# Turning input rows by DMA in two planes of 16-bit halves, in a hybrid attention and convolution layer

## The chip, the core and the metric

The kernel runs on one core of a Trainium2 chip, as one launch. The core has TensorE (matmuls, here also transposes), VectorE and ScalarE (element-wise work), GpSimd, and SyncE, which only issues DMAs. Each engine works through its own instruction list in order and waits at semaphores for the others. The metric is the device time of one execution in microseconds (us); lower is better.

## The reference

One layer on x of shape (1, 2048, 1024), all in float32:

```
h  = rms_norm(x, attn_norm_g)
z  = h @ w_in                     # q (512) k (128) v (128) gate_b gate_c xc (512 each)
q, k = rms_norm(q), rms_norm(k)   # per head of 64
A  = swa_sink_attention(q, k, v, sinks)      # window 128, 8 heads, 2 kv heads
Cv = gate_b * short_conv(gate_c * xc, conv_w)  # causal, 3 taps
x  = x + concat(rms_norm(A), rms_norm(Cv)) @ w_out
hm = rms_norm(x, mlp_norm_g)
x  = x + square(relu(hm @ w_up)) @ w_down      # 1024 -> 4096 -> 1024
```

## The kernel before

All products keep float32 accuracy by splitting each operand into a high part that TensorE takes at full rate and a low part (the remainder): three matmuls per product, high by high, high by low, low by high. ScalarE makes the high part (a copy with rounding), VectorE the low part (a subtraction).

The work comes in three stages. In the **mixers** (up to about 690 us) the 2048 positions are taken in four chunks of 512 rows, a chunk in four tiles of 128. For a chunk: projection to q, k, v; attention for the four tiles; the convolution branch in two halves (`conv_pair`, j = 0 and 1, each with products for gate_c, xc and gate_b); output projection in two halves (first the convolution's columns, then the attention's). Then come the **up projection** and the **down projection** over all rows, with a seven-product scheme for 2x2 blocks.

The order of the mixers is made by hand. `besides` is a generator: each `yield` ends one small piece of a chunk's convolution, output projection and preparation of the next chunk. The attention code calls `fill(n)`, which runs n such pieces; the table `FILL` holds the counts for each chunk, `PRIO` holds offsets to the priorities with which a scheduler then orders instructions on each engine. So attention's steps on ScalarE and VectorE are covered by filler matmuls on TensorE.

`prepare` makes the next chunk's operand h, which must have the model dimension on partitions. It loads a tile of 128 rows (`xt`, buffers for two), takes the sum of squares on ScalarE (`norm_stats`), the reciprocal root on GpSimd, scales on VectorE (`scaled`); then `transposed` turns it on TensorE, four 128x128 blocks into one PSUM bank (tag "tr", one buffer), and splits the bank into the high part (L310, ScalarE) and the low part (L311, VectorE) of h. It runs beside the first half of the output projection: after each piece of `prepare` come three pieces of the output projection (`STEPS`). The last chunk has no next one, so there are three such preparations, in chunks 0, 1 and 2, of 4 tiles each.

Of the kernel before, what the change touches and what calls it, by code (L numbers as in the profile page):

```python
# [10 lines left out]
I32 = mybir.dt.int32  # L11
AF = mybir.ActivationFunctionType
# [55 lines left out]
PC = (2, 1)  # L68

# [8 lines left out]
LATE_RSTD = (  # L78
    (3, 3),
    (2, 2),  # L80
)
# [5 lines left out]
PRIO = (  # L87
# [5 lines left out]
)  # L93

FILL = (
# [4 lines left out]
)  # L100
# [4 lines left out]
def hymba_layer(  # L105
# [168 lines left out]
    last_sum = [None]  # L274

# [23 lines left out]

    def transposed(xt, dst, t, name, tag="tr"):  # L300

        for kk in range(0, KD, 4):
            with ahead(9):
                pt = bank(tag, f"pt_{name}_{kk}")
                for j in range(4):
                    nc.tensor.transpose(pt[:, j * P : (j + 1) * P], xt[:, (kk + j) * P : (kk + j + 1) * P], ident)
                p3 = pt.rearrange("p (k t) -> p k t", k=4)
                dh = dst[0][:, kk : kk + 4, t * P : (t + 1) * P]
                dl = dst[1][:, kk : kk + 4, t * P : (t + 1) * P]
                nc.scalar.copy(dh, p3)  # L310
                nc.vector.tensor_tensor(dl, p3, dh.bitcast(F32), op=ALU.subtract)  # L311
            yield
# [87 lines left out]
    def prepare(src, r0, gb, dst, name):  # L400

        xs = []

        def fetch(t):
            xt = row("xt", f"xt_{name}_{t}", 2)
            nc.sync.dma_start(xt, src[r0 + t * P : r0 + (t + 1) * P, :])
            with ahead(8):
                norm(xt, gb, f"{name}_{t}")
                xs.append(xt)
# [227 lines left out]
    with tc.tile_pool(name="mix_small", bufs=1) as mix_small, tc.tile_pool(name="mix", bufs=1) as mix:  # L637
# [193 lines left out]
        def attn_rstd(b, sqa, dst):  # L831
            pa = bank("tr", f"pa_b{b}")
            nc.tensor.matmul(pa[:, :1], sqa[:, :P], mean, start=True, stop=True)
            ms = small.tile([P, 1], F32, tag="ms", name=f"ms_b{b}", bufs=2)
            nc.vector.tensor_copy(ms, pa[:, :1])
            rsqrt(dst, ms)

        def conv_pair(c, h, j, yt, ssc):
# [30 lines left out]
            for i in range(2):  # L869
                ct = 2 * j + i  # L870
                ps = bank("mm", f"px_{nm}_{i}")
                yield from group(hl, ps, i)
                u = gc[i]
                with ahead(10):
                    nc.gpsimd.tensor_copy(u[:, :2], halo[:, ct, :])
                    nc.vector.tensor_tensor(u[:, 2 : CH + 2], ps, u[:, 2 : CH + 2], op=ALU.mult)
                    nc.gpsimd.tensor_copy(halo[:, ct, :], u[:, CH : CH + 2])
                    y = pool.tile([P, CHP], F32, tag="s2", name=f"y_{nm}_{i}", bufs=4)[:, :CH]
                    nc.vector.tensor_scalar(y, u[:, :CH], cw[:, ct, 0:1], None, op0=ALU.mult)
# [9 lines left out]
            for i in range(2):  # L889
# [4 lines left out]
                with ahead(10):  # L894
# [3 lines left out]
                    nc.scalar.copy(yh[:, 0], y)  # L898
# [28 lines left out]
        def out_projection(c, half, ys, rs, x1):  # L927

            for dh in range(2):
# [11 lines left out]
                for t, i in order:  # L941
# [17 lines left out]
                    if i < NCT - 1:  # L959
                        yield  # L960
                        continue
                    with ahead(11):
# [15 lines left out]
        def besides(c, before, h, yt, rc, x1, h_next, z_next):  # L978
# [3 lines left out]
            blocks = x_blocks() if c + 1 == NCHUNK else None  # L982
            for j in range(2):
# [12 lines left out]
            if c + 1 < NCHUNK:  # L996
                h_next += parts(pool, "h", f"h{c + 1}")
                steps = prepare(xf, (c + 1) * CH, g_row[0], h_next, f"a{c + 1}")
            else:
                steps = range(PC[0] + 1)  # L1000
            for i, _ in enumerate(steps):
                yield
                for j in range(STEPS):
                    next(out, None)
                    yield
                    if (i, j) == PC:
                        pc = bank("tr", f"pc{c}")
# [603 lines left out]
```

## Time and profile before

| | |
|---|---|
| runs | 1914.98, 1916.66, 1916.91 us; median 1916.66 |
| profiled execution | span 1913.4 us from the first to the last instruction; the page gives no other time of its own |
| TensorE matmuls | 8930, busy 1907.7 us |
| VectorE, ScalarE, GpSimd busy | 1202.7, 829.4, 274.4 us |
| granted TensorE clock | 1.000 over the core's span |
| DMA | 413.80 MB, mean 216 GB/s |

The profile is that of one execution. A line like `L310 ACT CAST h_h<-pt_a` names the code line, the engine (PE is TensorE, PEld its weight loads, DVE VectorE, ACT ScalarE, POOL GpSimd, SP SyncE), the operation, and what it writes and reads. Groups give total busy time and the mean length of one in ns. Busy shares average over stages with different limits, so the stage is looked at by itself.

### The profile page before, as it was taken

The page shows a single profiled execution, that of the slowest core. Times are in us where ns is not written, and L with a number is a line of the kernel's source. Part 1 is how long each engine was busy: PE and PEld are TensorE (multiplying, and loading weights), DVE is VectorE, ACT ScalarE, POOL GpSimd, SP SyncE. Part 2 cuts the span into 40 slices and gives each one's busy share as a digit, 9 for nine tenths or more (in the row PEclk, how much of TensorE's full clock was granted, in tenths as well). Part 3 has the DMA queues.
Part 4 walks back from the last instruction along what each step waited for, and adds up shares of the span by engine and source line. Part 5 has one row for each costly group of instructions (what it writes and reads, how often), then busy time and mean ns, then how long its engine had stood idle before and what let it go on. Part 6 is the DMA issues. An engine that isn't in the chain of part 4 may idle for free.

```text
span 1913.4 us, 24557 instructions
## 1 busy us (share of the span) xinstructions
PE 1907.7 (100%) x8930; PEld 1591.1 (83%) x8930; DVE 1202.7 (63%) x1857; ACT 829.4 (43%) x1557; POOL 274.4 (14%) x477
## 2 busy tenths in 40 slices
PE   9999999999999999999999999999999999999999
PEld 8888888888888888888888888888888888888887
DVE  5895567448467759998788766666534334457531
ACT  6564245335445346544555545453332332232320
POOL 2123212302221112233101111111000000100000
PEclk9999999999999999999999999999999999999999
DMA  9984844564578688777576544448954457766631
GB/s 305 333 320 120 329 189 177 213 227 160 203 266 277 215 294 251 221 215 244 195 233 213 175 145 159 140 148 321 364 198 150 138 171 224 281 228 213 217 124 55
DMA packets 232792, 413.80 MB, mean 216 GB/s; under 512 B 51672, under 2 KB 136416, under 8 KB 219872
## 3 DMA queue, kind: packets, MB, share of 16 engines
q1 hardware_dynamic: 203840, 336.59, 52.0%
q0 software_dynamic: 15424, 51.40, 6.9%
q10 hardware_dynamic: 13408, 24.26, 3.4%
q8 instruction: 70, 1.15, 0.2%
q14 instruction: 50, 0.41, 0.1%
HBM read 286.35 MB, written 125.83 MB: 215 GB/s over the span
## 4 chain that ended last, share of the span: by engine, by line
PE 99%; DVE 0%; POOL 0%; issue 0%; ACT 0%; DVEq 0%; POOLq 0%
PE u L1454 32%; PE d L1571 32%; PE pout L278 3%; PE pout L280 3%; PE pout L279 3%; PE pz L278 2%; PE pz L280 2%; PE pz L279 2%; PE psc_b L724 2%; PE pb_c L280 2%; PE pb_c L279 2%; PE pb_c L278 2%; PE px_c L278 2%; PE px_c L279 2%; PE px_c L280 2%; PE po_b L812 1%
## 5 line engine op out<-in xcount | busy, mean ns | idle before, releaser
L1454 PE MATMUL u<-op_x,wop 128*128 128x512 f32 x2688 | 609.7, 389 | 0.0
L1571 PE MATMUL d<-op_w,op_f 128*128 128x512 f32 x2691 | 609.5, 389 | 0.0
L1571 PEld LDWEIGHTS d<-op_w,op_f 128*128 128x128 f32 x2691 | 504.8, 188 | 104.7
L1454 PEld LDWEIGHTS u<-op_x,wop 128*128 128x128 f32 x2688 | 504.3, 188 | 105.3 <-issue 0.3
L434 DVE TENSOR_TENSOR op_f<-op_f 128x1024 fp32r<-128x1024 f32 x112 | 136.8, 1224 | 235.6 <-ACT op_f L433 235.4
L433 ACT CAST op_f<-op_f 128x1024 fp32r<-128x1024 f32 x112 | 117.7, 1051 | 349.5 <-DMA op_f<-fop 349.0
L452 ACT CAST wop<-wu 128x512 fp32r<-128x512 f32 x156 | 96.1, 619 | 92.0 <-PE u L1454 88.3
L453 DVE TENSOR_TENSOR wop<-wu,wop 128x512 fp32r<-128x512 f32 x156 | 110.2, 708 | 31.8 <-ACT wop L452 16.7
L1190 POOL DMA_DIRECT2D fop<-s x96 | 52.1, 542 | 443.2 <-DVE s L1193 436.7
L1196 DVE TENSOR_TENSOR u<-u,u 128x512 f32<-128x512 f32 x128 | 87.7, 685 | 19.4 <-PE u L1454 19.2
L434 DVE TENSOR_TENSOR op_w<-raw,op_w 128x1024 fp32r<-128x1024 f32 x56 | 68.3, 1221 | 28.8 <-ACT op_w L433 28.8
L433 ACT CAST op_w<-raw 128x1024 fp32r<-128x1024 f32 x56 | 58.8, 1052 | 48.4 <-PE d L1571 26.3
L1202 ACT ACTIVATE u<-u 128x512 f32<-128x512 f32 x64 | 40.5, 632 | 56.5 <-DVE u L1196 54.3
L741 ACT ACTIVATE sc_b<-sc_b,ngm_b 128x128 f32<-128x128 f32 x128 | 49.7, 389 | 30.0 <-DVE ngm_b L738 30.0
L773 POOL TENSOR_SCALAR_AFFINE_SELECT pp_b<-pp_b 128x512 fp32r<-128x512 f32 x60 | 41.3, 701 | 134.6 <-ACT pp_b L766 66.1
L1403 POOL DMA_DIRECT2D wds<-raw x16 | 8.5, 533 | 329.9 <-DVE raw L1401 329.9
L453 DVE TENSOR_TENSOR wop<-wu_s,wop 128x512 fp32r<-128x512 f32 x64 | 45.9, 718 | 11.9 <-ACT wop L452 11.7
L452 ACT CAST wop<-wu_s 128x512 fp32r<-128x512 f32 x64 | 39.4, 620 | 29.3 <-PE u L1454 24.9
L278 PE MATMUL pout<-w_wo,yt_c 128*128 128x512 f32 x128 | 51.5, 402 | 0.0
L280 PE MATMUL pout<-w_wo,yt_c 128*128 128x512 f32 x128 | 51.0, 398 | 0.0
L279 PE MATMUL pout<-w_wo,yt_c 128*128 128x512 f32 x128 | 50.2, 393 | 0.0
L735 DVE COPY_PREDICATED sc_b<-later,psc_b 128x128 f32<-128x128 int32 x120 | 29.4, 296 | 32.0 <-ACT sc_b L732 31.7
(265 smaller groups left out, 3119.0 us busy)
## 6 DMA issues: line engine op xcount, KB each, us to landing
op_f<-fop SPq DMA_DIRECT2D x112, 512.0 KB, 4.3
raw<-in_w_down_dram SPq DMA_DIRECT2D x72, 512.0 KB, 4.1
wu<-in_w_up_dram SPq DMA_DIRECT2D x128, 256.0 KB, 3.8
w_wo<-wo SPq DMA_DIRECT2D x24, 1024.0 KB, 6.7
fop<-s POOLq DMA_DIRECT2D x96, 256.0 KB, 2.6
fop<-u ACTq DMA_DIRECT2D x64, 256.0 KB, 2.6
op_x<-xop SPq DMA_DIRECT2D x28, 512.0 KB, 6.0
w_q<-q SPq DMA_DIRECT2D x12, 1024.0 KB, 6.7
```

The lines of the kernel that those rows point to most:

```text
L278: nc.tensor.matmul(ps, st(0), mv(0), start=first, stop=False)
L279: nc.tensor.matmul(ps, st(0), mv(1), start=False, stop=False)
L280: last_sum[0] = nc.tensor.matmul(ps, st(1), mv(0), start=False, stop=last).ins
L433: nc.scalar.copy(op[:, 0], raw)
L434: nc.vector.tensor_tensor(op[:, 1], raw, op[:, 0].bitcast(F32), op=ALU.subtract)
L452: splits.append(nc.scalar.copy(hi, blk).ins)
L453: lows.append(nc.vector.tensor_tensor(lo, blk, hi.bitcast(F32), op=ALU.subtract).ins)
L741: nc.scalar.activation(sc[:, hd, :], sc[:, hd, :], AF.Exp, bias=ngm[:, hd : hd + 1], accum_out=den[:, hd : hd + 1])
L1190: eng.dma_start(fop_dram[tb][ORDER_DOWN.index(i)][n // 2][:, n % 2], b)
L1196: return nc.vector.tensor_tensor(dst, ps, b, op=ALU.add).ins
L1454: nc.tensor.matmul(pt, wops[i][:, a, k, :], xops[tb, p][k // 2][:, b, k % 2, :], start=p not in GOES_ON and k + j == 0, stop=k + j == NB + ...
L1571: nc.tensor.matmul(ps[tb][j][:, cs], fs[tb][:, a, k, j * P : (j + 1) * P], w[:, b, k, cs], start=first and p not in GOES_ON and k + n == 0 ...
```

## The change

Chunks 1 to 3 no longer use TensorE to turn their rows. A row tile is loaded, squared and scaled as before. Then ScalarE copies the low and the high 16 bits of each 32-bit number into two planes (128 x 1024 halves each, strided reading); a DMA issued by ScalarE transposes the planes block by block back into the tile's own buffer (tiles 0 and 1: one DMA over both planes; tiles 2 and 3: one per plane); VectorE interleaves the turned halves into 32-bit numbers again, four copies of 512 halves per tile; and the high and low split follows from SBUF instead of PSUM. Tiles 0 and 1 start within the convolution branch (`EARLIER` gives the pieces of j = 1 after which the preparation's steps are taken), tiles 2 and 3 beside the output projection. The two parts of h are allocated after the second tile's interleaving. `behind` puts the new instructions behind the last gating steps of the convolution on ScalarE and VectorE. `FILL` and `PRIO` have new numbers. Chunk 0's own rows still go over TensorE.

```diff
+EARLIER = (16, 18, 23, 35, 38)
 ...
-    ((14, 15), (9, 9, 11, 8, 1), (9, 6, 8, 8, 2), (10, 11, 9, 8, 4), (13, 10, 7, 6, 1)),
+FILL = (((14, 15), (9, 9, 11, 8, 1), (9, 6, 8, 8, 2), (10, 11, 5, 8, 4), (11, 10, 9, 6, 0)),
 ...
+    def behind():
+        with tc.issue_after(gates["act"]), tc.issue_after(gates["dve"]):
+            yield
 ...
-    def transposed(xt, dst, t, name, tag="tr"):
-        for kk in range(0, KD, 4):
-            with ahead(9):
-                pt = bank(tag, f"pt_{name}_{kk}")
-                for j in range(4):
-                    nc.tensor.transpose(pt[:, j * P : (j + 1) * P], xt[:, (kk + j) * P : (kk + j + 1) * P], ident)
 ...
-                nc.scalar.copy(dh, p3)
-                nc.vector.tensor_tensor(dl, p3, dh.bitcast(F32), op=ALU.subtract)
-            yield
 ...
+        def halves(t):
+            if t < 2:
+                place = row("x1", f"half_{name}_{t}", NT)
+                places[t] = [place[:, i * BW : (i + 1) * BW] for i in range(2)]
+            else:
+                places[t] = [
+                    pool.tile([P, CHP], F32, tag="s2", name=f"half_{name}_{t}_{i}", bufs=4)[:, :BW] for i in range(2)
+                ]
+            xt = xs[t]
+            with ahead(8), behind():
+                scaled(xt, norm_stats(xt, f"{name}_{t}", junk=places[t][0]), gb)
+                pairs = xt.bitcast(U16).rearrange("p (c i) -> p i c", i=2)
+                for i, plane in enumerate(places[t]):
+                    nc.scalar.copy(plane.bitcast(U16), pairs[:, i])
+                turned_[t] = xt.bitcast(U16).rearrange("p (i k t) -> p i k t", i=2, k=KD)
+                if t < 2:
+                    out = xt.bitcast(U16).rearrange("p (k t) -> p k t", t=P)
+                    nc.scalar.dma_start_transpose(out, place.bitcast(U16))
+                else:
+                    for i, plane in enumerate(places[t]):
+                        nc.scalar.dma_start_transpose(turned_[t][:, i], plane.bitcast(U16))
+
+        def whole(t):
+            with ahead(9), behind():
+                for n, raw in enumerate(places[t]):
+                    pairs = raw.bitcast(U16).rearrange("p (k t i) -> p i k t", k=KH, i=2)
+                    for i in range(2):
+                        nc.vector.tensor_copy(pairs[:, i], turned_[t][:, i, n * KH : (n + 1) * KH])
+
+        def split(t):
+            with ahead(9), behind():
+                for n, raw in enumerate(places[t]):
+                    raw = raw.rearrange("p (k t) -> p k t", k=KH)
+                    dh, dl = (d[:, n * KH : (n + 1) * KH, t * P : (t + 1) * P] for d in dst)
+                    nc.scalar.copy(dh, raw)
+                    nc.vector.tensor_tensor(dl, raw, dh.bitcast(F32), op=ALU.subtract)
 
         fetch(0)
         fetch(1)
         yield
+        for t in range(2):
+            halves(t)
+            yield
+        for t in range(2):
+            whole(t)
+            fetch(t + 2)
+            yield
+        dst += parts(pool, "h", name)
         for t in range(NT):
-            yield from transposed(xs[t], dst, t, f"{name}_{t}")
-            if t + 2 < NT:
-                fetch(t + 2)
+            split(t)
+            if t < 2:
+                halves(t + 2)
+            if 0 < t < NT - 1:
+                whole(t + 1)
+            yield
 ...
+                    if j and not blocks and n in EARLIER:
+                        next(steps)
                     yield
```

On TensorE, in chunk 0's output projection (`pout_1_0_0`: convolution half, first 512 columns, tile 0), the program before has a group of four transposes between matmuls:

```order
L278 MATMUL pout_1_0_0_1461<-w_wo_0_1447,yt_c_1_0_1375 128x512
L279 MATMUL pout_1_0_0_1461<-w_wo_1_1448,yt_c_1_0_1375 128x512
L306 MATMUL pt_a_0_4_1519<-ident,xt_a_0_1427 128x128 x4
L280 MATMUL pout_1_0_0_1461<-w_wo_0_1447,yt_c_1_0_1375 128x512
L278 MATMUL pout_1_0_1_1509<-w_wo_0_1447,yt_c_0_0_969 128x512
```

and the changed one, at the same place (lines of the changed file):

```order
L274 MATMUL pout_1_0_0_1495<-w_wo_0_1481,yt_c_1_0_1411 128x512
L786 MATMUL ptp_b_0_1538<-ident,sc_b_995 128x128
L275 MATMUL pout_1_0_0_1495<-w_wo_1_1482,yt_c_1_0_1411 128x512
L786 MATMUL ptp_b_0_1538<-ident,sc_b_995 128x128
L276 MATMUL pout_1_0_0_1495<-w_wo_0_1481,yt_c_1_0_1411 128x512
```

The transposes of the rows are gone from there; those of the attention's probabilities (`ptp_b`), which exist in both programs, have come into this stretch.

On ScalarE, in the same stretch, the changed program has for tile 2 of the first preparation (`half_a_2_0` and `half_a_2_1` are its planes, `qt_b` and `kw` the turned q and k of the next attention tile):

```order
L403 COPY half_a_2_0_1467<-xt_a_2_1329 128x1024
L403 COPY half_a_2_1_1468<-xt_a_2_1329 128x1024
L283 ACTIVATE half_a_3_0_1509,ss_a_3_1511<-xt_a_3_1405 128x1024
L410 DMA_TRANSPOSE xt_a_2_1329<-half_a_2_0_1467 128x8x128
L410 DMA_TRANSPOSE xt_a_2_1329<-half_a_2_1_1468 128x8x128
L728 CAST qt_b_1638<-ptq_b_1639 64x4x128
```

Two copies and two transposing DMA issues now stand ahead of the cast of `qt_b`; before, casts out of `pt_a` stood among these instructions.

On VectorE the interleaving copies of that tile stand among the residual additions (`x_0_2`, `x_0_3`: the output projection's tiles 2 and 3 added to x):

```order
L991 SCALAR_TENSOR_TENSOR x_0_2_1457<-pout_1_0_2_1574,rc_661,x_0_2_1457 128x512
L290 SCALAR_TENSOR_TENSOR xt_a_3_1405<-xt_a_3_1405,rs_a_3_1513,g_attn 128x1024
L417 COPY half_a_2_0_1467<-xt_a_2_1329 128x512
L991 SCALAR_TENSOR_TENSOR x_0_3_1459<-pout_1_0_3_1615,rc_661,x_0_3_1459 128x512
L417 COPY half_a_2_0_1467<-xt_a_2_1329 128x512
L417 COPY half_a_2_1_1468<-xt_a_2_1329 128x512 x2
L729 TENSOR_TENSOR qt_b_1638<-ptq_b_1639,qt_b_1638 64x4x128
```

The first of these copies waits for the DMA, and the fourth residual addition and the low half of `qt_b` stand behind it; before, that place held the additions, the low halves and a subtraction out of `pt_a`.

More of the change, by code (lines that the diff above doesn't have):

```diff
@@ L1 @@
-from contextlib import ExitStack, nullcontext
+from contextlib import ExitStack, contextmanager, nullcontext
 import concourse.bass as bass
@@ L400, in prepare @@
     def prepare(src, r0, gb, dst, name):
-        xs = []
+        xs, places, turned_ = {}, {}, {}
         def fetch(t):
[L405 to L409, printed above, removed]
+            xs[t] = row("xt", f"xt_{name}_{t}", 2)
+            nc.sync.dma_start(xs[t], src[r0 + t * P : r0 + (t + 1) * P, :])
+        def halves(t):
[19 more added lines that the diff above has]
+                        nc.scalar.dma_start_transpose(turned_[t][:, i], plane.bitcast(U16))
@@ L897, in conv_pair @@
                     yt.append(yh)
[L898 removed]
+                    gates["act"] = nc.scalar.copy(yh[:, 0], y).ins
                     nc.vector.tensor_tensor(yh[:, 1], y, yh[:, 0].bitcast(F32), op=ALU.subtract)
@@ L961, in out_projection @@
                         continue
+                    assert (c, half, t) in factors
                     with ahead(11):
@@ L982, in besides @@
             blocks = x_blocks() if c + 1 == NCHUNK else None
+            if c + 1 < NCHUNK:
+                steps = prepare(xf, (c + 1) * CH, g_row[0], h_next, f"a{c + 1}")
+            else:
+                steps = range(PC[0] + 1)
             for j in range(2):
@@ L995, in besides @@
             out = out_projection(c, 1, yt, rc, x1)
[L996 to L1000, printed above, removed]
             for i, _ in enumerate(steps):
-                yield
+                if c + 1 == NCHUNK:
+                    yield
                 for j in range(STEPS):
@@ L1006, in besides @@
                     if (i, j) == PC:
+                        factors.update((c, 1, t) for t in range(NT))
                         pc = bank("tr", f"pc{c}")
```

21 lines of the change are left out of this document (9 added, 12 removed), and 8 rows, old and new, of tables (FILL, PRIO).

## The prediction

> **What bounds the kernel now.** I read the page first (busy shares, then the chain of waits), then the waits of each engine, and last the stretches round the transposes that are removed.
>
> ```profile
> span 1913.4 us, 24557 instructions
> PE 1907.7 (100%) x8930; PEld 1591.1 (83%) x8930; DVE 1202.7 (63%) x1857; ACT 829.4 (43%) x1557; POOL 274.4 (14%) x477
> PE 99%; DVE 0%; POOL 0%; issue 0%; ACT 0%; DVEq 0%; POOLq 0%
> ```
>
> TensorE is busy over the whole span, and the chain that ended last is TensorE for 99% of it. A busy share alone would not prove this, since matmul records overlap. The waits do: asked for TensorE's own waits from 30 to 700 us (all the mixers), the view has no row, while the other engines' lists are full of waits for TensorE. From 80 to 160 us ScalarE's list begins
>
> ```profile
> ACT o_b L820 <- PE po_b L812: 6.0, 1, 6.0
> ACT h_h L310 <- PE pt_a L306: 4.6, 5, 2.2
> ```
>
> So TensorE's instruction stream is the time (the chain in order of time has the up projection begin at 690.66 us, where the mixers end): whatever leaves the stream shortens it, whatever makes TensorE wait lengthens it. A matmul is counted by its spacing, not by its own length, and for the plain 128x512 product that is 609.7/2688 = 0.227 us:
>
> ```profile
> 690.66 609.56 PE u L1454 x2688
> L1454 PE MATMUL u<-op_x,wop 128*128 128x512 f32 x2688 | 609.7, 389 | 0.0
> ```
>
> **Removed: 96 transposes on TensorE.** All stand in the preparation of the next chunk's rows, in three bursts, in 24 groups of four.
>
> ```profile
> L306 PE MATMUL pt_a<-ident,xt_a x96: 270/272/329, 119.1 to 482.1; 128*128 128x128 f32 x96
> L306 PE MATMUL pt_a<-ident,xt_a 128*128 128x128 f32 x96 | 14.6, 274 | 0.0
> ```
>
> What one group costs the stream is read from the timeline, from the start of the matmul ahead of it to the start of the second matmul behind it:
>
> ```profile
> 121.48 0.39 PE L279 MATMUL pout<-w_wo,yt_c 128*128 128x512 f32 x1
> 121.71 0.60 PE L306 MATMUL pt_a<-ident,xt_a 128*128 128x128 f32 x4
> 122.06 0.48 PE L280 MATMUL pout<-w_wo,yt_c 128*128 128x512 f32 x1
> 122.37 0.40 PE L278 MATMUL pout<-w_wo,yt_c 128*128 128x512 f32 x1
> ...
> 143.62 0.39 PE L280 MATMUL pout<-w_wo,yt_c 128*128 128x512 f32 x1
> 143.85 0.60 PE L306 MATMUL pt_a<-ident,xt_a 128*128 128x128 f32 x4
> 144.21 0.48 PE L278 MATMUL pout<-w_wo,yt_c 128*128 128x512 f32 x1
> 144.52 0.40 PE L279 MATMUL pout<-w_wo,yt_c 128*128 128x512 f32 x1
> ```
>
> 122.37 - 121.48 = 0.89 us for two matmuls and the group; two matmuls are 0.454, so the group costs 0.44; at the second place 0.90 - 0.454 = 0.45. Mean 0.442 us, times 24 = **10.6 us**. The upper bound is the group's busy time, 14.6 us; the busy row counts the drain of the last transpose, under which the next matmul already runs, so I stay with 10.6.
>
> **Moved: the two splitting steps.** The 24 casts on ScalarE and 24 subtractions on VectorE remain, now reading SBUF. From PSUM they take 585 and 683 ns; the same shapes out of SBUF, in the up projection, 619 and 708:
>
> ```profile
> L310 ACT CAST h_h<-pt_a 128x512 fp32r<-128x512 f32 x24 | 14.0, 585 | 10.3 <-PE pt_a L306 10.2
> L311 DVE TENSOR_TENSOR h_h<-pt_a,h_h 128x512 fp32r<-128x512 f32 x24 | 16.4, 683 | 2.1 <-ACT h_h L310 2.0
> L452 ACT CAST wop<-wu 128x512 fp32r<-128x512 f32 x156 | 96.1, 619 | 92.0 <-PE u L1454 88.3 <-ACT u L1199 2.4 <-DVE wu L1176 1.3
> L453 DVE TENSOR_TENSOR wop<-wu,wop 128x512 fp32r<-128x512 f32 x156 | 110.2, 708 | 31.8 <-ACT wop L452 16.7 <-DMA wu<-in_w_up_dram 15.1
> ```
>
> That is 24 x 0.034 = 0.8 us on ScalarE and 24 x 0.025 = 0.6 us on VectorE, off the path. The rows' square-and-sum and scaling stay as they are, only earlier.
>
> **Added on ScalarE: 24 copies of 1024 16-bit halves and 18 transposing DMA issues.** No row has a 16-bit copy with a stride. The nearest of 1024 elements take 1051 to 1156 ns, so 24 x 1.05 = 25.2 us, 8.4 a chunk; if the chip moved two halves at once the 512-element row (619) would be the price, 14.9 in all. A plain DMA issue holds ScalarE for 0.326 us, so 18 are 5.9, 2.0 a chunk; a transposing one may hold it longer, which no row prices.
>
> ```profile
> L433 ACT CAST op_f<-op_f 128x1024 fp32r<-128x1024 f32 x112 | 117.7, 1051 | 349.5 <-DMA op_f<-fop 349.0 <-ACT f L1199 0.4
> L368 ACT ACTIVATE xt_m<-xt_m,rs_x 128x1024 f32<-128x1024 f32 x8 | 9.2, 1156 | 5.5 <-DMA xt_m<-x_dram 5.4
> L1190 ACTq DMA_DIRECT2D fop<-u x64: 326/326/362, 734.3 to 1302.5; - x64
> ```
>
> **Added on VectorE: 48 interleaving copies of 512 halves.** One-input work from SBUF of that length takes 484 ns, two-input work up to 708: 23.2 to 34.0 us, 7.7 to 11.3 a chunk. It is one-input work, so I take 484. Cover for both engines is read by stretch; the columns that matter are the third (VectorE) and fourth (ScalarE) busy time:
>
> ```profile
> L879 DVE TENSOR_SCALAR y_c<-u_c,cw 128x512 f32<-128x512 f32 x16 | 7.7, 484 | 0.9
> 60.00:110.00 50.00, 50.00 (x248) 41.94 (x247) 44.07 (x93) 28.77 (x83) 1.89 (x7) 1.00 0.91 346
> 110.00:150.00 40.00, 40.00 (x218) 34.08 (x217) 38.12 (x78) 26.80 (x72) 10.15 (x18) 1.00 0.72 260
> 150.00:180.00 30.00, 30.00 (x159) 25.30 (x158) 11.28 (x23) 10.91 (x29) 9.61 (x14) 1.00 0.26 89
> 280.00:310.00 30.00, 30.00 (x166) 25.49 (x165) 26.94 (x56) 19.13 (x52) 8.83 (x15) 1.00 0.42 159
> 310.00:340.00 30.00, 30.00 (x159) 25.67 (x158) 14.19 (x31) 12.24 (x36) 5.44 (x9) 1.00 0.35 135
> 450.00:480.00 30.00, 29.98 (x164) 24.97 (x162) 26.35 (x51) 18.78 (x47) 9.76 (x17) 1.00 0.45 170
> ```
>
> ScalarE is free for 90 - 55.6 = 34 us from 60 to 150, against 10.4 added: covered. VectorE is free there for 90 - 82.2 = 7.8 us, against 7.7 to 11.3: just covered, or 3.5 us over. In the second and third bursts half of a chunk's copies (rows 2 and 3, 3.9 to 5.7 us) fall into stretches with 3.1 and 3.65 us free: 0.8 to 2.6 and 0.2 to 2.0 over. In all **1.0 to 8.1 us** of VectorE's work is pushed into the stretch behind, where 18.7 and 15.8 us are free. TensorE pays for it only where something it needs soon stands behind, so nothing at the least; I take **2.0 us**, near the low end because the one-input price is the nearer one and not all that is late is urgent.
>
> **Added: a wait on VectorE for a DMA.** A row's first interleaving copy waits until its transposing DMA has landed, and VectorE works in order. For row 2 of the first burst, VectorE's order has the wait behind the third residual addition, and the issue on ScalarE stands just ahead of the cast of qt_b. Before, these two stood at
>
> ```profile
> 132.66 1.39 DVE L963 SCALAR_TENSOR_TENSOR x<-pout,rc,x 128x512 f32<-128x512 f32 x2
> ...
> 130.35 0.58 ACT L702 CAST qt_b<-ptq_b 64x512 fp32r<-64x512 f32 x1 [0.23 <-PE ptq_b L697]
> ```
>
> so from issue to need there are about 132.66 + 1.39 - 130.35 = 3.7 us. Behind the wait stand the fourth residual addition, which frees a PSUM bank of the output projection, and the low halves of qt_b and kw, which the scores on TensorE need. The landing is bounded by
>
> ```profile
> fop<-u ACTq DMA_DIRECT2D x64, 256.0 KB, 2.6
> xt_a<-in_x_dram SPq DMA_DIRECT2D x12, 512.0 KB, 4.4
> xt_r<-x_dram SPq DMA_DIRECT2D x32, 128.0 KB, 3.9
> ```
>
> Plain, half a row (256 KB) lands in 2.6 us and a whole one in 4.4: no wait, or 0.7 us. The last row is the nearest to short pieces (128 KB in runs of 32 words); at its rate a whole row of halves, 512 KB, takes 4 x 3.9 = 15.6 us. I take 4.4: the transfer stays in SBUF, and outside the first burst the DMA engines are less than half busy (0.42 and 0.45 above).
> [...]
>
> **Sum.** 1913.4 - 10.6 + 2.0 = 1904.8 us of span. The page names no time beside the span; the median of the runs, 1916.66, stands 3.3 above it, and I keep that: **1908 us**, 0.45% faster. The up and down projections (from 690 us on) keep their instructions and their order, and move earlier as a block.
>
> **Rivals.**
> 1. *VectorE becomes the bound in the three bursts.* The copies cost the two-input price, and all 8.1 us of overrun reach TensorE: 1916.7 - 10.6 + 8.1 = 1914, no change. For it: 38.12 of 40 us busy from 110 to 150. Against it: 11.28 of 30 behind it, and TensorE does not wait once today although VectorE is as full.
> 2. *The transposes were cover.* They filled TensorE while the attention's softmax ran elsewhere; without them 3.5 us a chunk come back as waits: 1916 to 1917, no change. Against it: the wait rows above, in which ScalarE waits for TensorE and not the reverse, so the chain has room.
> 3. *Slow landing, the other side.* At 15.6 us a row VectorE stands for 15.6 - 3.7 = 11.9 us at row 2, and again at row 3, 24 us a chunk. If filler hides half, TensorE loses 12 us in each of three chunks: 1916.7 - 10.6 + 36 = 1942, slower. It decides from 10.6/3 = 3.5 us lost a chunk, thus from a landing of about 7 us where nothing hides it. For it: the DMA share of 0.91 and 0.72 in the first burst, where transfers must share. Against it: 0.42 and 0.45 in the two others.
>
> **How the numbers follow.** Forecast 0.70; rival 1, 0.10; rival 2, 0.05; rival 3, with milder forms that still end above 1920, 0.15. The first is faster by over 0.2% (3.8 us, about what a measurement of this kernel can tell from no change), the next two are within it, the last is slower: 0.70, 0.15, 0.15. The forecast's own range is 1904 (no overrun, a little over 10.6 saved) to 1912 (6 us of the overrun paid). To hold eight in ten it reaches over rivals 1 and 2 to 1917; rival 3 stays outside.
>
> **What would show it.** In the changed profile: TensorE's count down by 96 and, from 30 to about 680 us, next to no rows for TensorE in the waits; the first up-projection matmul near 682 instead of 690 us; interleaving copies near 0.48 us; transposing DMAs landing in 3 to 5 us. Wrong would be: waits of VectorE for xt_a of several us each (rival 3), TensorE waiting for VectorE with VectorE full behind 110 us (rival 1), or for ScalarE's exponentials (rival 2).

## The result and the profile after

The changed kernel takes 1943.66 us (median of 4 runs, 1939.94 to 1950.68) against 1916.09 before, a ratio of 1.0148 (95% interval 1.0128 to 1.0168): 27.6 us slower, where 1908 us was predicted. The page of the changed kernel, and from its chain in order of time (start, length, engine, line) the two projections:

```profile
span 1941.2 us, 24490 instructions
PE 1911.1 (98%) x8834; PEld 1588.8 (82%) x8834; DVE 1221.1 (63%) x1905; ACT 850.4 (44%) x1581; POOL 281.7 (15%) x477
...
718.49 609.61 PE u L1485 x2688
1328.10 609.32 PE d L1602 x2691
```

TensorE has its 96 matmuls less, and still the up projection starts at 718.49 us instead of 690.66: all 27.8 us are lost in the mixers. The view of TensorE's waits from 30 to 700 us, which had no row before, now has (total us, times, longest):

```profile
PE pout L274 <- DVE x L991: 8.0, 2, 4.4
PE po_b L838 <- POOL pp_b L799: 5.6, 6, 2.9
PE psc_b L750 <- DVE qt_b L729: 5.1, 1, 5.1
PE pout L275 <- DVE w_wo L247: 1.6, 1, 1.6
```

Three waits lead: the output projection for a residual addition (`x`) that frees its bank, the values product for the masked probabilities (`pp_b`), the scores for the low half of the turned q (`qt_b`). A second loss shows in the stretches; the last columns are granted clock, DMA share and GB/s:

```profile
110.00:150.00 40.00, 29.23 (x121) 23.67 (x122) 27.48 (x55) 23.83 (x59) 8.54 (x13) 0.83 0.88 231
365.00:385.00 20.00, 16.52 (x97) 14.33 (x96) 13.43 (x23) 9.70 (x22) 11.72 (x13) 0.91 0.57 237
485.00:512.00 27.00, 22.22 (x94) 17.57 (x93) 17.23 (x41) 12.97 (x32) 2.54 (x5) 0.87 0.77 223
```

A mean of 0.83 over 40 us is 13.6 us at half clock; with 3.6 and 7.0 us in the other rows about 24 us (in windows of 1 us it reads 0.50, from 113 to 119 us for one; the clock's own record adds up to 23.9), where before the clock was 1.000 throughout. TensorE's timeline shows what that does behind a wait:

```profile
501.08 0.39 PE L276 MATMUL pout<-w_wo,yt_c 128*128 128x512 f32 x1
505.89 0.80 PE L274 MATMUL pout<-w_wo,yt_c 128*128 128x512 f32 x1 [4.43 <-DVE x L991]
506.49 0.63 PE L275 MATMUL pout<-w_wo,yt_c 128*128 128x512 f32 x1
506.91 0.63 PE L276 MATMUL pout<-w_wo,yt_c 128*128 128x512 f32 x1
```

Starts are 0.42 us apart instead of 0.227 (0.427 over the stretch). In 3.2 of the 23.9 us at half clock TensorE stood idle anyway (2.5 us in the gap before 115.12 us, 0.7 in the one before 505.89), so the half clock loses 20.7 x 0.200/0.427 = 9.7 us. Of the gaps between matmul starts 15 are over 0.5 us longer than the usual spacing; they add up to 27.2 us. 27.2 + 9.7 - 10.6 for the transposes = 26.3 of the 27.8 us; 1.5 us stay open.

The new operations themselves, by tile (least/median/longest ns), with one row of VectorE's waits and one of the landings (median us):

```profile
L417 DVE COPY half_a<-xt_a x48: 421/452/909, 109.1 to 514.5; 128x512 uint16<-128x512 uint16 x48
L403 ACT COPY half_a<-xt_a x24: 1030/1042/1049, 88.4 to 494.7; 128x1024 uint16<-128x1024 uint16 x24
L410 ACTq DMA_TRANSPOSE xt_a<-half_a x12: 1247/1346/7220, 139.6 to 497.2; - x12
L407 ACTq DMA_TRANSPOSE xt_a<-half_a x6: 1595/2137/9789, 90.9 to 463.5; - x6
...
DVE half_a L417 <- DMA xt_a<-half_a: 9.7, 5, 3.1
...
xt_a<-half_a ACTq DMA_TRANSPOSE x18, 4.8
```

The copies cost what was forecast, and half of the transfers land within 4.8 us; the longest recorded landing, of the row issued at 90.94 us, takes 18.2. The issues are far longer than forecast: one holds ScalarE for up to 9.79 us. At the longest, ScalarE's, VectorE's and TensorE's timelines read

```profile
103.93 9.79 ACTq L407 DMA_TRANSPOSE xt_a<-half_a  x1
113.76 0.58 ACT L728 CAST qt_b<-ptq_b 64x512 fp32r<-64x512 f32 x1 [8.34 <-issue]
114.37 0.69 DVE L729 TENSOR_TENSOR qt_b<-ptq_b,qt_b 64x512 fp32r<-64x512 f32 x1 [4.43 <-ACT qt_b L728]
115.12 3.36 PE L750 MATMUL psc_b<-kw,qt_b 128*128 128x256 f32 x14 [5.12 <-DVE qt_b L729]
```

The second cast of `qt_b` stands behind the issue, VectorE's low half behind the cast, the scores behind that; the next 14 matmuls run at half clock (0.50 until 119.5 us).

### The profile page after: what moved, and what is told of

Same layout as the page of the kernel before. It is cut to its first block, busy times and chain, and to the rows that moved or that the text cites. A ratio compares the mean times of both kernels' runs of the same rounds, so it can differ in the third digit from the quotient of the medians.

```text
span 1941.2 us, 24490 instructions
## 1 busy us (share of the span) xinstructions
PE 1911.1 (98%) x8834; PEld 1588.8 (82%) x8834; DVE 1221.1 (63%) x1905; ACT 850.4 (44%) x1581; POOL 281.7 (15%) x477
## 4 chain that ended last, share of the span: by engine, by line
PE 80%; DVE 1%; ACT 1%; POOL 1%; ACTq 1%; issue 0%; DMA 0%; DVEq 0%
PE u L1485 31%; PE d L1602 31%; PE pout L274 2%; PE pout L275 2%; PE pout L276 2%; PE pz L274 1%; PE pz L276 1%; PE pz L275 1%; PE px_c L274 1%; PE px_c L276 1%; PE px_c L275 1%; PE pb_c L274 1%; PE pb_c L276 1%; PE po_b L838 1%; PE pb_c L275 1%; PE pc_c L275 1%
## 5 line engine op out<-in xcount | busy, mean ns | idle before, releaser
L274 PE MATMUL pout<-w_wo,yt_c 128*128 128x512 f32 x128 | 53.2, 418 | 8.4 <-DVE x L991 8.0
L750 PE MATMUL psc_b<-kw,qt_b 128*128 128x256 f32 (+1 forms) x256 | 51.6, 292 | 6.0 <-DVE qt_b L729 5.1
L275 PE MATMUL pout<-w_wo,yt_c 128*128 128x512 f32 x128 | 52.3, 409 | 1.6 <-DVE w_wo L247 1.6
L479 DVE TENSOR_TENSOR wop<-wu_s,wop 128x512 fp32r<-128x512 f32 x64 | 45.9, 718 | 12.3 <-ACT wop L478 12.2
```

Source lines behind the costliest of these rows:

```text
L274: nc.tensor.matmul(ps, st(0), mv(0), start=first, stop=False)
L275: nc.tensor.matmul(ps, st(0), mv(1), start=False, stop=False)
L479: lows.append(nc.vector.tensor_tensor(lo, blk, hi.bitcast(F32), op=ALU.subtract).ins)
L750: nc.tensor.matmul(ps[:, j].rearrange("p s k -> p (s k)")[:, :nk], qt[:, pr, j, :], kw[:, r, kv, :, :].rearrange("p s k -> p (s k)")[:, :n ...
```

## The experiments

All times are medians, each against its own runs of the kernel before (1915.5 to 1916.6).

| run | us | against before | ratio, 95% interval |
|---|---|---|---|
| changed kernel | 1943.66 | +27.6 | 1.0128 to 1.0168 |
| e1 no transposing DMA | 1933.98 | +18.5 | 1.0079 to 1.0109 |
| e2 issued by SyncE | 1931.95 | +16.5 | 1.0070 to 1.0100 |
| e3 no interleaving | 1960.35 | +44.8 | 1.0206 to 1.0251 |
| e5 no weight stores | 1946.45 | +31.0 | 1.0147 to 1.0181 |
| e6 old tables | 1957.67 | +42.0 | 1.0202 to 1.0236 |
| e7 kernel before, new tables | 1952.69 | +37.0 | 1.0173 to 1.0204 |
| e4 first rows on TensorE | 1929.71 | +14.0 | 1.0061 to 1.0091 |
| e8 SyncE, old tables | 1930.21 | +14.5 | 1.0054 to 1.0084 |
| e9 before, no transposes | 1913.58 | -2.3 | 0.9978 to 0.9997 |
| e10 e9 and plane copies | 1918.53 | +2.7 | 1.0002 to 1.0022 |
| e11 e9 and interleaving | 1928.07 | +12.2 | 1.0047 to 1.0077 |
| e12 SyncE, GpSimd interleaves | 1928.29 | +12.0 | 1.0048 to 1.0082 |
| e13 SyncE, filler corrected | 1919.75 | +3.2 | 1.0008 to 1.0026 |
| e14 e13, old priorities | 1918.09 | +1.5 | 1.0001 to 1.0020 |
| e15 e14, GpSimd interleaves | 1916.19 | -0.4 | 0.9991 to 1.0009 |
| e16 filler corrected alone | 1948.51 | +31.9 | 1.0137 to 1.0188 |
| e17 e13, first rows on TensorE | 1911.88 | -3.8 | 0.9978 to 0.9996 |
| e18 e17, old priorities, GpSimd | 1918.01 | +2.3 | 1.0008 to 1.0025 |

### Are the issue holds the loss?

The theory was that ScalarE's holds make the stalls; the rivals, that the new order of the work or VectorE's copies do. e1 leaves the transposing DMAs out (the copies stay and read unturned rows), e2 only has SyncE issue them:

```diff
-                    nc.scalar.dma_start_transpose(out, place.bitcast(U16))
+                    nc.sync.dma_start_transpose(out, place.bitcast(U16))
 ...
-                        nc.scalar.dma_start_transpose(turned_[t][:, i], plane.bitcast(U16))
+                        nc.sync.dma_start_transpose(turned_[t][:, i], plane.bitcast(U16))
```

> Leaves out the 18 transposing DMAs alone: the ScalarE copies into planes, the VectorE interleaving copies (they read the unturned tile, halves taken from alternate places), the order tables and everything else stay. Theory H (ScalarE is held while a transposing DMA is handed to busy DMA engines: 4.1 and 9.8 us in the first burst, 7.2 us in the third; VectorE and then TensorE wait for it and the TensorE clock halves after each longer gap): the 8.3, 8.4 and 3.1 us waits of ScalarE for issue vanish, with them the TensorE gaps at 110 and 501 us (5.4 and 4.8) and at 142 (4.0), and most of the half clock; time 1908 to 1916. Theory V (the added copies fill VectorE and ScalarE): still 1935 or more. Theory O (the new order tables expose attention's chain): 1925 to 1935, with the gaps at 142 and 374 us left.

> The same transposing DMAs are issued by SyncE instead of ScalarE. Theory H: ScalarE has no issue waits, SyncE shows the holds instead; SyncE only prefetches, so time 1910 to 1922. If it is the landing of the turned row that VectorE waits for, and not the hold of ScalarE, the time stays at 1935 to 1945 with VectorE's waits for the DMA grown. If the weight loads behind the held SyncE queue come late, TensorE or ScalarE show waits for DMA in the mixers and the time is above 1945.

Without the DMAs 9.7 us come back, with SyncE issuing them 11.7. The holds are a real part of the loss, and SyncE can bear them, but 16.5 us are left: the theory explains less than half. e1's time lies in the range expected if the new order tables were the cause (Theory O), which the next section tests. In e1's list of TensorE's waits the same three waits lead, with no transposing DMA in the program:

```profile
PE po_b L832 <- POOL pp_b L793: 5.7, 7, 2.9
PE psc_b L744 <- DVE qt_b L723: 5.6, 1, 5.6
PE pout L274 <- DVE x L985: 4.7, 2, 3.1
```

e3 leaves out the interleaving copies (both planes then take the upper halves, and the split reads the row's buffer directly):

```diff
-                    for i in range(2):
-                        nc.vector.tensor_copy(pairs[:, i], turned_[t][:, i, n * KH : (n + 1) * KH])
+                    pass
 ...
-                for n, raw in enumerate(places[t]):
-                    raw = raw.rearrange("p (k t) -> p k t", k=KH)
+                for n in range(2):
+                    raw = xs[t][:, n * BW : (n + 1) * BW].rearrange("p (k t) -> p k t", k=KH)
```

> Leaves out the 48 interleaving copies on VectorE: the split reads the turned tile as it lies (both planes hold the upper halves, so that all numbers are finite). The DMAs and their issue on ScalarE stay. Theory V (VectorE is the bound in the bursts): 1905 to 1915. Theory H: the holds of ScalarE are unchanged, and so is most of the loss: 1932 to 1944.

It became 16.7 us slower than the changed kernel, outside both ranges. It doesn't tell what it was made for: the wait for the landing moved from VectorE's copies to ScalarE's cast, in front of the attention's work on ScalarE; TensorE's waits in e3 have one of 9.1 us for `qt_b` and one of 8.0 for ScalarE's copy of the scores (`sc_b`).

e5 asks what makes a hold long. It leaves out the stores of split weights in chunk 0 but one, whose bytes later chunks then read:

```diff
+        if parts_dram:
+            parts_dram[name] = parts_dram["qkv2"]
+            return
```

> Leaves out the stores of the split weights in the first chunk but for the first one (later chunks load that one's bytes in place of each other's), so that the DMA engines are freer in the first burst. If a transposing DMA holds ScalarE because it shares the DMA engines with other traffic, the holds at 91 and 104 us fall from 4.1 and 9.8 us to near the 1.6 us of the quiet second burst, the TensorE gap of 5.4 us at 110 us vanishes, and the time falls by 8 to 18 us to 1926 to 1936; the 7.2 us hold of the third burst stays. If the hold is a fixed cost, nothing changes: 1940 to 1948.

The issues that held ScalarE for 4.12 and 9.79 us took 1.71 and 1.64 in e5. The stretch from 90 to 114 us, of the changed kernel and then of e5, and e5's two issues:

```profile
90.00:114.00 24.00, 20.00 (x96) 16.28 (x94) 13.52 (x22) 9.41 (x17) 2.16 (x4) 0.97 1.06 305
```

```profile
90.00:114.00 24.00, 24.00 (x122) 20.05 (x121) 20.79 (x43) 16.08 (x31) 2.33 (x4) 1.00 0.50 137
...
91.87 1.71 ACTq L410 DMA_TRANSPOSE xt_a<-half_a  x1
103.54 1.64 ACTq L410 DMA_TRANSPOSE xt_a<-half_a  x1
```

At a DMA share of 0.50 instead of 1.06 TensorE doesn't wait there at all (24.00 of 24 us busy). So these two holds were short once the stores were gone. The time did not fall: later gaps of 3.6, 2.8 and 3.3 us (133 to 157 us) took the place of the one removed. The second of them stands behind a hold again, of 6.80 us for two half rows, in ScalarE's timeline of e5:

```profile
142.68 6.80 ACTq L413 DMA_TRANSPOSE xt_a<-half_a  x2
149.53 0.58 ACT L726 CAST qt_b<-ptq_b 64x512 fp32r<-64x512 f32 x1 [6.29 <-issue]
```

Before the third, VectorE waits 3.30 us for that row to land. So e5 shows that the traffic of the stores made two holds long, but not what the holds cost; e1 and e2 do, and they leave most of the loss to something else.

### Is it the tables?

e6 gives the changed kernel the FILL and PRIO of the kernel before, e7 the reverse, e8 is e6 with SyncE issuing; e4 turns chunk 1's rows on TensorE with chunk 0's old table rows.

```diff
-PRIO = ((60, 0, 160, -130, 30, 0, 20, -10, 0, 0, 0, 300, 0, 10), ...
+PRIO = ((60, 0, 160, -10, 30, 0, 20, -10, -20, 30, 0, 300, 0, 0), ...
-FILL = (((14, 15), (9, 9, 11, 8, 1), (9, 6, 8, 8, 2), (10, 11, 5, 8, 4), (11, 10, 9, 6, 0)), ...
+FILL = (((14, 15), (9, 9, 11, 8, 1), (9, 6, 8, 8, 2), (10, 11, 9, 8, 4), (13, 10, 7, 6, 1)), ...
```

> The changed kernel with FILL and PRIO of the kernel before; everything else (planes, transposing DMAs on ScalarE, interleaving, EARLIER) stays as changed. Theory T (the refitted tables make the steady stalls, those at 202, 212, 309, 331, 371, 374, 542 and 551 us that every variant so far showed and the kernel before does not have): these go, about 7.6 us of gaps and 3.4 us of half clock, so 1929 to 1936; the stalls behind the issue holds at 104 and 497 stay. Rival S (the stalls come from the change's structure: the preparation no longer gives the attention its pieces of filler, and its work stands on ScalarE and VectorE at other places; the tables were fitted to soften that): 1945 or more, with stalls at other places. Rival N: the tables do nothing, 1941 to 1946.

> The kernel before with FILL and PRIO of the changed one; rows still turned by TensorE. Theory T: the stalls at about 202, 212, 309, 371 and 551 us appear here too, 1922 to 1932. Rival S: the tables by themselves cost nothing, 1914 to 1919, no stall over 0.5 us in TensorE's stream.

> The changed kernel with both: SyncE issues the transposing DMAs (1931.95 by itself) and FILL and PRIO of the kernel before. Theory T: the two parts add, 1918 to 1925. Rival S: 1932 or more. If the removed transposes' 10.6 us were all gained and no stall stayed: 1905.

```diff
-            if c + 1 < NCHUNK:
+            if 0 < c and c + 1 < NCHUNK:
 ...
+            if not c:
+                h_next += parts(pool, "h", f"h{c + 1}")
+                steps = prepare_pe(xf, (c + 1) * CH, g_row[0], h_next, f"a{c + 1}")
```

> The rows of chunk 1, which are prepared in chunk 0, go over TensorE as before, with chunk 0's rows of FILL and PRIO of the kernel before; chunks 2 and 3 by DMA as changed. If the loss is made in the first burst (gaps of 12.1 us between 109 and 160 us and about 10 us of half clock, less the 3.5 us of transposes that come back): 1924 to 1928. If the first burst's loss only shows there what is made elsewhere (a backlog that then appears in the second burst): 1932 or more. The stalls at 374 and 501 us stay in either case.

Theory T fell. The old tables make the changed kernel 14 us slower still, the new ones make the kernel before 37 us slower: each table fits its own structure, and that is no sign that either fits well. With SyncE issuing, both do about alike (1931.95 and 1930.21, between what T and its rival expected), and the wait of `po_b` at the end of chunk 1 (3.2 us at 374 us) is in every variant so far that has the new preparation. e4 gained 14 us, somewhat less than if the first burst alone made its losses (1924 to 1928).

### What each part costs by itself

Three runs take the kernel before apart. e9 leaves out the 96 transposes and puts nothing in their place (cast and subtraction read the scaled, unturned rows); e10 adds to that the 24 plane copies, e11 the 48 interleaving copies, both into buffers that nobody reads (the three edits in this order).

```diff
-                pt = bank(tag, f"pt_{name}_{kk}")
-                for j in range(4):
-                    nc.tensor.transpose(pt[:, j * P : (j + 1) * P], xt[:, (kk + j) * P : (kk + j + 1) * P], ident)
-                p3 = pt.rearrange("p (k t) -> p k t", k=4)
+                p3 = xt[:, kk * P : (kk + 4) * P].rearrange("p (k t) -> p k t", k=4)
 ...
+                for i in range(2):
+                    nc.scalar.copy(junk[:, :BW].bitcast(mybir.dt.uint16), pairs[:, i])
 ...
+                for i in range(2):
+                    nc.vector.tensor_copy(pairs[:, i], u16[:, kk // 4 + 2 * i])
```

> The kernel before without its 96 transposes and nothing in their place: cast and subtraction read the scaled rows themselves, unturned, so h holds other numbers. It prices the first term of the sum by itself. Theory P (TensorE's stream is the time, the term holds): 1905 to 1908. Theory C (the transposes were cover for the attention: in the kernel before the last filler matmul of a chunk stands only 3 to 6 us behind the attention's last values product, 359 against 356 us in chunk 1): part or all of the 3.5 us a chunk comes back as waits for pp_b or o_b at the chunks' ends, 1910 to 1917.

> The run without the transposes, and in it the 24 plane copies on ScalarE alone (written to a buffer that nobody reads; no DMA, no interleaving). Theory A (ScalarE's 8.4 us a chunk stand ahead of attention's casts and exponentials and delay its chain, so TensorE runs out of filler at the chunks' ends): slower than the run without the transposes by 6 to 25 us, with waits for pp_b at the chunks' ends. Rival (ScalarE has room, 34 us free in the first burst): within 2 us of it.

> The run without the transposes, and in it the 48 interleaving copies on VectorE alone (from the scaled rows into a buffer that nobody reads; no DMA, no plane copies). Theory D (VectorE, with 7.8 us free in the first burst, is what delays the attention): slower than the run without the transposes by 4 to 20 us, most in the first burst. Rival (off the path): within 2 us of it; my prediction had 2.0.

Of the 10.6 us only 2.3 are gained (0.6 to 4.2 by the interval). The execution of e9 that was profiled is 5.3 us faster than the median of before, and has seven gaps of over 0.5 us between matmul starts, 5.4 us in all beyond the usual spacing: together about the 10.6. Its waits are spread over six causes, the longest 1.0 us, so they bear out Theory C's size more than its place. The plane copies cost 5.0 us, a little less than the least expected, and not where Theory A had it: TensorE's waits for `pp_b` in e10 are 0.5 us in all. The interleaving copies cost 14.5. In e10 and e11 the buffers that nobody reads come from the pool of the attention's `o_b`, so a part of both costs can be a lack of buffers and not engine time; no run separates that. Of the largest wait in e11, VectorE's and then TensorE's timeline show how it comes about:

```profile
482.89 1.27 DVE L294 SCALAR_TENSOR_TENSOR xt_a<-xt_a,rs_a,g_attn 128x1024 f32<-128x1024 f32 x1
484.08 1.21 DVE L739 TENSOR_REDUCE ngm_b<-sc_b 128x8 f32<-128x1024 f32 x1
485.21 0.78 DVE L308 COPY half_a<-xt_a 128x512 uint16<-128x512 uint16 x2
485.88 0.68 DVE L313 TENSOR_TENSOR h_h<-xt_a,h_h 128x512 fp32r<-128x512 f32 x1
486.48 0.78 DVE L308 COPY half_a<-xt_a 128x512 uint16<-128x512 uint16 x2
487.16 0.68 DVE L313 TENSOR_TENSOR h_h<-xt_a,h_h 128x512 fp32r<-128x512 f32 x1
...
487.83 0.74 DVE L965 SCALAR_TENSOR_TENSOR x<-pout,rc,x 128x512 f32<-128x512 f32 x1
```

```profile
488.63 0.79 PE L278 MATMUL pout<-w_wo,yt_c 128*128 128x512 f32 x1 [4.44 <-DVE x L965]
```

The residual addition that frees the output projection's bank stands behind row work that nobody needs yet (and one step of the attention, L739); TensorE waits 4.44 us for it, though VectorE has some room over the burst as a whole. e12 is e2 with the interleaving copies on GpSimd:

```diff
-                        nc.vector.tensor_copy(pairs[:, i], turned_[t][:, i, n * KH : (n + 1) * KH])
+                        nc.gpsimd.tensor_copy(pairs[:, i], turned_[t][:, i, n * KH : (n + 1) * KH])
```

> The changed kernel with the transposing DMAs on SyncE (1931.95 by itself) and the 48 interleaving copies on GpSimd in place of VectorE. Theory D (VectorE's added work is the largest loss, 14.5 us when added alone to the run without the transposes): 1917 to 1922. Rival G (GpSimd's copies are slow and stand ahead of its work for the attention, the masks of pp_b and the reciprocal roots): 1932 or more, TensorE waiting for POOL. A result below 1914 would need the transposes' full 10.6 us and is not expected by either.

3.7 us better than e2, neither theory's figure. Either the 14.5 us belong to the places of the copies in e11 more than to VectorE's load, or GpSimd's slower copies (768 ns in the median against 452 on VectorE in the changed kernel) take back a part; this run doesn't separate them. The wait for `pp_b` stood as before.

### The filler that ran out

The chunk's end has the common wait. TensorE's timeline there, of the kernel before and of the changed one:

```profile
351.67 0.63 PE L812 MATMUL po_b<-pp_b,vz 128*128 128x512 f32 x2
352.13 0.62 PE L812 MATMUL po_b<-pp_b,vd 128*128 128x512 f32 x2
352.60 0.28 PE L278 MATMUL pz<-w_qkv,h_h 128*128 128x256 f32 x1
```

```profile
373.41 0.60 PE L723 MATMUL ptq_b<-ident,z 128*128 128x128 f32 x4
373.84 0.27 PE L725 MATMUL ptk_b<-ident,z 128*128 128x128 f32 x1
373.87 0.48 PE L838 MATMUL po_b<-pp_b,vz 128*128 128x512 f32 x1
377.29 0.49 PE L838 MATMUL po_b<-pp_b,vd 128*128 128x512 f32 x1 [2.94 <-POOL pp_b L799]
```

Before, behind the first values product of the chunk's last tile comes the next chunk's projection (`pz`), until 359 us. In the changed kernel nothing is left, and TensorE waits for GpSimd's mask. The generator's pieces, counted as the program is built:

```
chunk   asked for in the last two fills   got      left over behind them
before: 0    6, 1                         6, 1     6
        1    5, 3                         5, 3     4
        2    5, 2                         5, 2     8
after:  0    6, 0                         6, 0     2
        1    5, 2                         4, 0     0
        2    5, 1                         5, 1     4
```

`prepare` used to give nine pieces a chunk to the filler. Its first five steps are now taken inside the convolution's pieces (`EARLIER`) and the last four yield no piece, so nine are gone; the rows of FILL ask for 5, 2 and 5 fewer (174, 211 and 204 in place of 179, 213 and 209). The rest comes out of the chunk's tail, where the cover is needed. e13 is e2 with FILL of the kernel before, less exactly those nine pieces in the calls in which they stood (chunks 0 to 2):

```diff
+FILL = (((14, 15), (9, 9, 11, 8, 1), (9, 6, 7, 6, 1), (10, 9, 9, 8, 4), (10, 10, 7, 6, 1)),
+        ((25, 15), (9, 16, 11, 8, 1), (9, 8, 13, 2, 1), (13, 9, 13, 6, 5), (7, 14, 11, 5, 3)),
+        ((20, 17), (9, 16, 11, 9, 1), (9, 5, 11, 6, 1), (16, 6, 12, 6, 6), (7, 15, 10, 5, 2)), ...
```

e14 takes PRIO (and FILL's last row) of the kernel before as well, e15 adds GpSimd's copies to that, e16 is the changed kernel with the corrected FILL alone.

> Transposing DMAs on SyncE (1931.95 by itself); FILL for chunks 0 to 2 is that of the kernel before with the nine pieces of the preparation taken off in the calls in which they stood, so the real filler lies where it lay and 6, 4 and 8 pieces are left behind the last values product; PRIO as changed. Theory F (filler used up too early makes the stalls at the chunks' ends: 8.5 us of gaps and 3.4 of half clock with SyncE issuing): 1920 to 1925. Rival M (the attention's chain is late by the added work, wherever the filler lies; the stalls move to the bursts): 1929 or more.

> The same with PRIO, and FILL's last row, of the kernel before. Theory F: 1918 to 1925, as the priorities then put attention where it stood. Rival M: 1928 or more (1930.21 with the old FILL as it was).

> The same as the run ahead of it, and the interleaving copies on GpSimd. If F and VectorE's work are two separate causes, they add: 1914 to 1920, the floor being the 1918.5 of the run with plane copies alone, or 1913.6 without any added work. Rival M: 1926 or more.

> The changed kernel with the corrected FILL alone, issues still on ScalarE. Theory F: the stalls at 202, 212, 310, 374, 377 and 551 us go (8 us and 3.4 of half clock), 1931 to 1936. Rival M: 1941 or more.

A table of counts brings 12.2 us. The wait for `pp_b` in TensorE's list, of e2 and then of e13:

```profile
PE po_b L838 <- POOL pp_b L799: 5.8, 7, 3.0
```

```profile
PE po_b L838 <- POOL pp_b L799: 0.9, 1, 0.9
```

e14 and e15 go the same way, down to no difference from before. e16 missed: the waits at the chunks' ends go there too, but in the first burst a hold grew in their place. ScalarE's and TensorE's timeline of e16:

```profile
135.74 10.87 ACTq L410 DMA_TRANSPOSE xt_a<-half_a  x1
146.65 0.58 ACT L728 CAST qt_b<-ptq_b 64x512 fp32r<-64x512 f32 x1 [11.16 <-issue]
```

```profile
161.38 1.23 PE L750 MATMUL psc_b<-kw,qt_b 128*128 128x256 f32 x4 [11.38 <-DVE qt_b L729]
```

Two issues behind it held ScalarE for another 8.17 us. So the two causes don't simply add: while the issues are on ScalarE, better filler buys nothing. Why the hold grew is not shown. In e13 chunk 2 already takes 163.5 us instead of 167.3 (from the end of one chunk's output projection to the next's): all of a chunk's 3.5 us are gained there; chunk 1 takes 171.1 instead of 171.9. Chunk 0 ends at 218.4 instead of 211.9. e17 therefore is e13 with chunk 1's rows on TensorE again, as in e4; e18 is e17 with the old PRIO and last FILL row and GpSimd's copies.

> Rows of chunk 1 (prepared in chunk 0) over TensorE as in the kernel before, with its rows of FILL and PRIO for chunk 0; rows of chunks 2 and 3 by DMA, issued by SyncE, FILL for chunks 1 and 2 with the pieces taken off where they stood, PRIO for chunks 1 to 3 as changed. If the quiet bursts gain and the first one made the loss: chunk 0 ends at 212 us as before, chunks 1 and 2 take 171.1 and 163.5 us as in the run with the corrected filler, 1911 to 1914, faster than before. If the loss moves on to chunk 1, whose attention then starts with less of its work done: 1916 to 1922.

> The same with PRIO and FILL's last row of the kernel before, and the interleaving copies of chunks 2 and 3 on GpSimd. If VectorE's work in the quiet bursts still costs: 1909 to 1913. If GpSimd's copies delay its masks (one wait of 2.5 us for pp_b at 263 us in the run with corrected filler and GpSimd): 1914 to 1918.

e17 is the fastest kernel of this study: 1911.88 us, 0.9987 (0.9978 to 0.9996). Chunks 1 and 2 took 171.1 and 163.5 us, as expected, and TensorE's list of waits is down to two rows:

```profile
PE pout L276 <- DVE x L1027: 1.7, 2, 1.6
PE pa_b L895 <- DVE o_b L890: 0.4, 1, 0.4
```

e18 shows where GpSimd's copies can hurt: four of them, 2.75 us in all, stand ahead of its mask, which comes late (GpSimd's timeline, and TensorE's wait).

```profile
262.79 2.75 POOL L433 COPY half_a<-xt_a 128x512 uint16<-128x512 uint16 x4 [2.02 <-ACT qt_b L764]
265.46 0.63 POOL L835 TENSOR_SCALAR_AFFINE_SELECT pp_b<-pp_b 128x512 fp32r<-128x512 f32 x1
...
PE po_b L874 <- POOL pp_b L835: 3.2, 1, 3.2
```

e18 has the old priorities as well, so the 6.1 us between it and e17 are not the copies' alone; from e14 to e15, where only the copies moved, the time fell by 1.9 us, little more than the intervals can tell.

## Why the prediction was wrong

**Transposes removed, 10.6 us.** Right as TensorE work (gain and gaps of e9), wrong as time. The prediction let every microsecond that leaves TensorE's stream shorten the program, because TensorE never waited; e9 shows 2.3. A stream without waits says that the others keep up, not by how much. That is near rival 2, with a chance of 0.05; in e9 by itself its size (1916 to 1917) was nearer than the term's.

**Splits and copies.** The prices held: cast 618 ns (619 forecast), subtraction 681 (708), plane copy 1042 (1050), interleaving copy 452 (484). "Covered" did not hold: the plane copies cost 5.0 us in e10, though ScalarE had 34 us free from 60 to 150 us. Free time summed over a stretch doesn't show whether an instruction stands ahead of one that is urgent.

**Issues, 18 x 0.326 = 5.9 us.** Mis-sized. The 18 holds add up to 45 us, from 1.25 us for half a row to 9.79 for a whole one at a DMA share of 1.06 (from 90 to 114 us). The prediction said that no row priced it, then took the plain issue as the price and the sum as covered by ScalarE's free time, without an upper bound in the range. e2 prices it: 11.7 us.

**Stalls, 2.0 us (1.0 to 8.1).** The step that failed. It converted VectorE's overrun, a sum over a stretch, into TensorE's waits, and left out two things: what stands behind each new instruction on its engine (14.5 us in e11, where rival 1's bound was 8.1), and the filler. The diff shows that `prepare`'s yields disappear and FILL changes; the prediction had no term for it. e13 prices it at 12.2 us.

**Half clock.** Not foreseen: 9.7 of the lost microseconds are matmuls 0.427 us apart instead of 0.227, at a granted clock of 0.50, so here the gaps cost more than their length.

**Landing, 4.4 us.** Right in the median, 4.8, and VectorE waited 9.7 us in all for turned rows, not 24 a chunk. In the first burst one row landed only after 18.2 us and the next was first read 19.7 us after its issue, slower than rival 3 had it; but VectorE waited only 1.9 and 2.7 us for these two. Rival 3 gave 1942 us, nearly the time measured, by a mechanism that these runs exclude as the main loss (e1 has no landing to wait for and keeps 18.5 us of it); its number is a coincidence.

**Sum.** A run's time stands 1.7 us above its span (1942.91 against 1941.2), not 3.3: the profiled execution of before, 1915.1 by that, was among its shortest.

In order: 27.6 us of loss are 11.7 from the holds on ScalarE (e2), 12.2 from the filler once these are gone (e13), and 3.2 that are left; these go with the first burst's rows back on TensorE, which leaves a gain of 3.8 us (e17). The three add up to 27.1, as each run has its own runs of the kernel before. What of the 5.0 and 14.5 us of the copies lies in each of these shares was not separated; the copies' places differ. The 12.2 us hold for this order alone, since e16 has the same table and gains nothing.

## What to carry to other kernels

Count the pieces of filler that a change takes out of a hand-made order, and look at what covers the last dependent step of each stage: it runs out there, not where the work was removed. A transposing DMA's issue had a length of its own in these runs, 1.25 to 10.87 us where a plain issue took 0.326, and two of them (4.12 and 9.79 us) fell to 1.71 and 1.64 when other traffic was taken away; put it on a queue with nothing urgent behind it. Before adding up savings on an engine that never waits, take the work out alone and time it.

## What the runs showed of the hardware

A transposing DMA's issue held the engine that gave it. In the changed kernel ScalarE was held for 1.25 us with half a row (256 KB) and 1.60 with a whole one at the least, for up to 9.79 in a stretch with a DMA share of 1.06, and in e16 for 10.87 with half a row. SyncE was held in e12 for 1.24 to 2.48 us with half a row and 1.60 to 4.63 with a whole one. A plain issue on ScalarE took 0.326 in the kernel before. With half the share (0.50, e5) the two holds of the same stretch fell from 4.12 and 9.79 to 1.71 and 1.64 us. The share alone did not fix the length: at shares of 1.06, 1.08 and 1.02 while they lasted, the changed kernel's whole rows issued at 90.94, 103.93 and 447.56 us held ScalarE for 4.12, 9.79 and 2.63 us.

The granted clock fell to 0.50 in five stretches of the changed kernel's mixers, of 6.83 us (from 112.6 and 505.2 us) and 3.41 us (from 129.7, 146.8 and 378.9 us); in the kernel before it was 1.000 over the span. Four of the five came with gaps of 3.2 to 5.3 us in TensorE's stream (in two of these the half clock began while TensorE still stood), one followed gaps of 1.8 and 0.6.
